# Attention heads taken in pairs, with the masks added by VectorE, in a two-block network on one core

## The chip, the cores and the metric

The kernel runs on one core of a Trainium2 chip. The metric is the device time of one execution in microseconds (us), taken as the median of repeated runs. The engines are named as in the profile: PE is TensorE (matmuls), PEld its weight load, DVE is VectorE, ACT is ScalarE, POOL is GpSimd and SP is the engine that issues most of the DMAs.

## What is computed

Two transformer-like blocks are computed one after the other on 512 tokens of width 1024, in float32. The change touches only the attention of the first block, which has two kinds of heads, eight of each:

```python
def causal_dense_attention(q, k, v, scale):      # 8 heads, d = 96, values of 64
    s = einsum('bqhd,bkhd->bhqk', qi, k) * scale
    s = where(kpos <= qpos, s, NEG_INF)
    p = softmax(s, axis=-1)
    return einsum('bhqk,bkhd->bqhd', p, v)

DIL_PATTERNS = ((128, 1), (512, 4), (2048, 16))
def dilated_attention(q, k, v):                  # 8 heads, d = 64
    for window, dil in DIL_PATTERNS:
        o, lse = banded_causal_attention(strided q, k, v, window // dil)
    w = softmax(stack(lses)); return sum(w * outs)

mix = concatenate([o_mla, o_dil]) @ w_o
x = x + g1 * mix
h2 = rms_norm(x, g_ffn_norm) * (1 + sc2) + sh2   # then a gated FFN, then block 2
mod = silu(c) @ w_ada + b_ada                    # gives sh1, sc1, g1, sh2, sc2, g2
```

The kernel computes the three dilated patterns as one softmax over all keys: a key that lies in k patterns gets the logarithm of k added to its score, and a key that lies in none a large negative number. So both kinds of heads are a score matrix, an additive mask that depends on query and key alone, a softmax, and a product with the values.

## The kernel before, in words

The work before the attention makes the queries and keys transposed (`qT`, `kT` for the causal heads, 96 rows of a head on the partitions; `qd`, `kd` for the dilated heads, where an even head lies on partitions 0 to 63 and the odd one on 64 to 127 of one tile) and the values (`vm`, `vd`). The attention is written as a software pipeline in `block1`: step `n` of 18 makes the scores of head `n`, then transposes the probabilities of head `n-1`, then multiplies those of head `n-2` with the values. A scheduler that builds the program may move instructions of an engine past each other; the order that comes out is fixed when the program is built.

`scores` (lines 404 to 427) works on four query tiles of 128. Tile `i` sees `n = (i+1)*128` keys. L411 is the matmul of queries and keys into a PSUM tile `pp`. A mask matmul then adds the mask into the same tile: for causal heads L708 (an identity matrix times `cmR`, 128 columns, on the diagonal tile alone), for dilated heads L711 and L712 (identity times the high and the low part, `dmH` and `dmL`, of the dilated mask, all `n` columns each). L414 takes the negative row maximum on DVE (`nmax`), L417 the exponential on ACT out of PSUM into SBUF (`probs`), which also gives the row sum `den` by a second ACT instruction; L419 is the reciprocal (`rden`) on DVE. L423 (ACT, tiles 2 and 3) and L425 (DVE, tiles 0 and 1) scale the rows by it.

`probs_T` (lines 429 to 445): ten 128x128 transposes on PE (L438) into three PSUM tiles `aux`, copied to SBUF (`ptr`) by DVE (L441, 512 columns) and ACT (L443, 512 and 256 columns). `attend` (lines 447 to 449): four matmuls (L449, 512, 384, 256 and 128 columns) into 64 partitions of the PSUM tile `pv`, the lower 64 for an even head, the upper 64 for an odd one. After each second head `pv` is split (`split`, L131 on ACT and L132 on DVE) into `mixH` and `mixL`, the two parts that the product with `w_o` (`mm3`, L126 to L128, three matmuls for one product) takes.

All L411, L438 and L449 matmuls are float32 and run as two passes each, so a row of the profile says x2 for one of them, x10 for five transposes' passes, x8 for the four of `attend`. The pools: four PSUM banks for `pp`, three for `aux`, one for `pv`; two `ptr` buffers of 1,280 columns.

Between the heads runs `ada_tiles` (lines 267 to 283), a generator of which each step of the pipeline takes one: it loads 1 MB of `w_ada` (L273, tile `wada`), and DVE multiplies it with a column of silu(c) and adds it to `acc` (L275 for the first of eight, L277 for the others). After eight steps 16 matmuls of one column each (L281, 32 passes) sum `acc` over the partitions, and L282 adds the bias. Two such groups run here. Behind the attention come the small constants of block 2 (`s5_poles`, L898 to L985, mostly DVE on 64x64 tiles), and the product with `w_o` with its weight splits (`wh` by ACT, L131; `wl` by DVE, L132), its evictions (L767) and the first product of the FFN.

Of the kernel before, what the change touches and what calls it, by code (L numbers as in the profile page):

```python
# [11 lines left out]
F32 = mybir.dt.float32  # L12
# [7 lines left out]
P = 128  # L20
# [49 lines left out]
class Kern:  # L70
# [15 lines left out]
    def raw(self):  # L86
        """The next landing place of a weight load."""
# [52 lines left out]
    def rsqrt_act(self, out, ss, n, tag):  # L140
        """out <- (ss / n + EPS) ** -0.5: square root, reciprocal, one Newton step."""
# [11 lines left out]
    def rsqrt_dve(self, out, ss, n, tag):  # L153
        """out <- (ss / n + EPS) ** -0.5 by a bit estimate and three Newton steps."""
# [14 lines left out]
    def later(self, lag, fn):  # L169
        """Queue fn to be traced after the next lag products."""  # L170
# [96 lines left out]
    def ada_tiles(self, c0, n, dst, acc):  # L267
        """dst <- columns c0.. of silu(c) @ w_ada + b_ada, one column per 128; a generator of its steps."""
# [16 lines left out]
    def bcast_rows(self, dst, rstd, n):  # L285
        """dst [P, n*128] <- rstd[:, t] of token t*128+p, on every partition."""
# [8 lines left out]
    def sumsq_add(self, kt, acc, sq, x, e=None):  # L295
        """acc <- acc + x * x, feature tile by feature tile."""
# [7 lines left out]
    def sumsq_rows(self, ps, acc, t0, sizes):  # L304
        """Per token sums over the partitions of acc: column t0 + i of ps for the i-th token tile."""
# [5 lines left out]
    def rstd_rows(self, ps, cols, rb):  # L311
        """rb, on every partition: the reciprocal roots of the mean squares of the tokens in cols; ps: their sums of squares."""
# [17 lines left out]
    def scale_split(self, H, L, x, g):  # L330
        """H, L <- the two parts of x * g, g per partition."""
# [3 lines left out]
    def modulate(self, tiles, src, rb, G, sh, H, L):  # L335
        """H, L <- the two parts of src * rb * G + sh, feature tile by feature tile."""
# [52 lines left out]
    def rope(self, out, x, key, t, heads, rstd):  # L389
        """out, x: [P, heads, d] views; rstd [P, heads]."""  # L390
# [1255 lines left out]
```

## Time and profile before

| | us |
|---|---|
| median of three runs | 1876.71 |
| lowest and highest of them | 1876.2, 1882.28 |
| span of the profiled execution | 1874.8 |
| attention, first score matmul to the first product after the last ones matmuls (216.9 to 346.2) | 129.3 |
| the stretch behind it, up to the transposes of block 2's constants (346.2 to 402.3) | 56.1 |

The profiled execution shows a span of 1874.8 us, from its first to its last instruction; the profile gives no other time of that execution, so what lies around the span is taken as the difference to the median, 1.9 us. In the rows below times are in us from the start of the span; "x8" counts instructions; "idle before" is what the engine waited for. [...]

### The profile page before, as it was taken

What the parts mean: (1) busy time and instruction counts of PE and PEld (TensorE: products, weight loads), DVE (VectorE), ACT (ScalarE), POOL (GpSimd) and SP (SyncE); (2) the same over time, 40 slices, a digit from 0 to 9 for tenths busy, and PEclk for the clock granted to TensorE, in tenths of its full rate; (3) what the DMA queues carried; (4) which work ended last, traced back from release to release, by engine and by line L of the source; (5) the groups of instructions that cost most, each with busy time, mean ns of one, the idle gap of its engine ahead of it and who ended that gap; (6) DMA issues with size and microseconds to landing.
All of it is one profiled execution on the core that took longest, in us unless ns stands there. A gap on an engine that the chain in (4) does not pass through costs nothing. (4 is left out here: it accounts for less than half of the span.)

```text
span 1874.8 us, 28652 instructions
## 1 busy us (share of the span) xinstructions
PE 1796.3 (96%) x11605; PEld 1570.5 (84%) x11605; DVE 1079.9 (58%) x2281; ACT 785.1 (42%) x1290; POOL 320.8 (17%) x440
## 2 busy tenths in 40 slices
PE   1989999999999999999799999999999999999998
PEld 1777765787777777889799999999999999989996
DVE  5697857787543465554488334442444476536652
ACT  3674555345432343333545645342322444324432
POOL 5000000058763861012000000110000000000001
PEclk9899999999999999999899899999999999999999
DMA  7332524343334335355722244824643322332231
GB/s 272 107 111 93 187 91 135 110 78 125 96 112 124 129 116 155 112 188 99 185 74 91 71 135 150 183 97 160 216 139 113 102 91 68 102 107 95 69 102 45
DMA packets 178767, 226.66 MB, mean 121 GB/s; under 512 B 10699, under 2 KB 146746, under 8 KB 175178
## 3 DMA queue, kind: packets, MB, share of 16 engines
q1 hardware_dynamic: 164256, 181.95, 30.6%
q0 software_dynamic: 10640, 38.19, 7.6%
q10 hardware_dynamic: 3738, 4.69, 0.7%
q8 instruction: 91, 1.49, 0.3%
q14 instruction: 42, 0.34, 0.1%
HBM read 196.29 MB, written 32.70 MB: 122 GB/s over the span
## 5 line engine op out<-in xcount | busy, mean ns | idle before, releaser
L126 PE MATMUL pp<-s,wh 128*128 128x258 f32 (+2 forms) x1856 | 533.2, 287 | 2.3 <-DVE st L1206 1.0
L127 PE MATMUL pp<-s,wh 128*128 128x258 f32 (+2 forms) x1856 | 531.6, 286 | 0.0
L128 PE MATMUL pp<-s,wl 128*128 128x258 f32 (+2 forms) x1856 | 529.4, 285 | 0.0
L132 DVE TENSOR_TENSOR wl<-wraw,wh 128x1024 fp32r<-128x1024 f32 (+4 forms) x264 | 307.6, 1178 | 193.8 <-ACT wh L131 192.8
L131 ACT CAST wh<-wraw 128x1024 fp32r<-128x1024 f32 (+4 forms) x264 | 249.1, 965 | 365.9 <-PE pp L127 232.4
L126 PEld LDWEIGHTS pp<-s,wh 128*128 128x128 f32 x1856 | 355.9, 192 | 5.1 <-issue 1.6
L127 PEld LDWEIGHTS pp<-s,wh 128*128 128x128 f32 x1856 | 356.6, 192 | 0.3 <-DVE s L333 0.2
L128 PEld LDWEIGHTS pp<-s,wl 128*128 128x128 f32 x1856 | 356.5, 192 | 0.0
L126 PE MATMUL pp<-h2H,wh 128*128 128x512 f32 x336 | 134.2, 400 | 2.4 <-DVE cy L852 2.4
L127 PE MATMUL pp<-h2L,wh 128*128 128x512 f32 x336 | 133.8, 398 | 0.8 <-DVE h2L L343 0.7
L128 PE MATMUL pp<-h2H,wl 128*128 128x512 f32 x336 | 132.6, 395 | 0.0
L126 PEld LDWEIGHTS pp<-h2H,wh 128*128 128x128 f32 x336 | 63.4, 189 | 20.2 <-ACT aH L131 2.8
L127 PEld LDWEIGHTS pp<-h2L,wh 128*128 128x128 f32 x336 | 63.4, 189 | 16.0 <-DVE h2L L343 2.0
L128 PEld LDWEIGHTS pp<-h2H,wl 128*128 128x128 f32 x336 | 63.6, 189 | 14.4
L126 PE MATMUL pp<-aH,wh 128*128 128x512 f32 x176 | 70.1, 398 | 0.0
L127 PE MATMUL pp<-aL,wh 128*128 128x512 f32 x176 | 69.8, 396 | 0.0
L128 PE MATMUL pp<-aH,wl 128*128 128x512 f32 x176 | 69.8, 396 | 0.0
L1563 POOL TENSOR_TENSOR ht<-ht,gf 128x512 f32<-128x512 f32 x4 | 5.7, 1434 | 344.7 <-ACT fsq L1561 344.7
L126 PE MATMUL pp<-wh,hH 128*128 128x512 f32 (+1 forms) x160 | 62.7, 392 | 1.2 <-ACT hH L519 1.2
L127 PE MATMUL pp<-wl,hH 128*128 128x512 f32 (+1 forms) x160 | 62.2, 388 | 0.5 <-DVE wl L132 0.5
L1527 DVE TENSOR_TENSOR xz<-pp,rb_f 128x516 f32<-128x516 f32 x44 | 30.6, 696 | 54.3 <-PE pp L128 54.3
L128 PE MATMUL pp<-wh,hL 128*128 128x512 f32 (+1 forms) x160 | 61.5, 385 | 0.0
(598 smaller groups left out, 3566.1 us busy)
## 6 DMA issues: line engine op xcount, KB each, us to landing
wraw<-in_w_up_dram SPq DMA_DIRECT2D x40, 1024.0 KB, 5.8
wada<-in_w_ada_dram SPq DMA_DIRECT2D x24, 1024.0 KB, 5.0
wraw<-in_w_in_dram SPq DMA_DIRECT2D x17, 1024.0 KB, 6.0
wraw<-in_w_in_dram SPq DMA_DIRECT2D x26, 512.0 KB, 6.3
wraw<-in_w_down_dram SPq DMA_DIRECT2D x16, 704.0 KB, 4.5
wraw<-in_w_down_dram SPq DMA_DIRECT2D x8, 1024.0 KB
xraw<-MO_d SPq DMA_DIRECT2D x5, 896.0 KB
sg_d<-sg POOLq DMA_DIRECT2D x16, 258.0 KB, 2.4
```

What stands on the lines that cost most here:

```text
L126: mm(ps, lhsT=sh, rhs=mh, start=start, stop=False)
L127: mm(ps, lhsT=sh, rhs=ml, start=False, stop=False)
L128: mm(ps, lhsT=sl, rhs=mh, start=False, stop=stop)
L131: self.nc.scalar.copy(H, x)
L132: self.nc.vector.tensor_tensor(L, x, H.bitcast(F32), ALU.subtract)
L1527: nc.vector.tensor_tensor(xz, ps, rb, ALU.mult)
L1563: nc.gpsimd.tensor_tensor(h, h, gf[:, :512], ALU.mult)
```

## The change

The heads are taken in pairs, so the pipeline has 10 steps. `scores` makes the tiles of the two heads in turn: tile `i` of the first, tile `i` of the second, each into its own `pp` bank. There is no mask matmul. DVE reads the scores from PSUM and the mask from SBUF and writes minus their sum to SBUF, with the running minimum as `nmax` in the same instruction (`tensor_tensor_reduce`); the exponential then reads that SBUF tile in place, with a scale of -1. The causal mask is now a tile of 512 columns of which 384 are zero, the dilated one a single float32 tile. `attend` takes the two heads in turn: the first writes partitions 0 to 63 of `pv`, the second 64 to 127. The `ptr` tiles live in the weight pool, under the tags `wh` and `wl` of the weight splits, and `probs` has four buffers of each size instead of two. Two steps of `ada_tiles` are taken for each pair.

In the diff the comments that were only deleted are left out.

```diff
-    def scores(self, qT, kT, mask):
+    def scores(self, pair, mask):
         nc = self.nc
-        probs = []
+        probs = ([], [])
         for i in range(NT):
             n = (i + 1) * P
-            sc = self.prod()
-            nc.tensor.matmul(sc[:, :n], lhsT=qT[:, i * P : (i + 1) * P], rhs=kT[:, :n], start=True, stop=False)
-            mask(sc, i, n)
-            nm = self.tmp.tile([P, 1], F32, tag="nmax", bufs=8, name=self.nm("nmax"))
-            nc.vector.tensor_reduce(nm, sc[:, :n], AX.X, ALU.max, negate=True)
-            pr = self.att.tile([P, n], F32, tag=f"probs{i}", bufs=2, name=self.nm("probs"))
-            nc.scalar.activation(pr, sc[:, :n], AF.Exp, bias=nm, scale=1.0, accum_out=den)
+            scs = [self.prod() for _ in pair]
+            for (qT, kT), sc in zip(pair, scs):
+                nc.tensor.matmul(sc[:, :n], lhsT=qT[:, i * P : (i + 1) * P], rhs=kT[:, :n], start=True, stop=True)
+            for a, sc in enumerate(scs):
+                nm = self.tmp.tile([P, 1], F32, tag="nmax", bufs=16, name=self.nm("nmax"))
+                pr = self.att.tile([P, n], F32, tag=f"probs{i}", bufs=4, name=self.nm("probs"))
+                nc.vector.tensor_tensor_reduce(pr, sc[:, :n], mask[:, S - n :], -1.0, 3.0e38, ALU.add, ALU.min, nm)
+                nc.scalar.activation(pr, pr, AF.Exp, bias=nm, scale=-1.0, accum_out=den)
...
-    def probs_T(self, probs):
+    def probs_T(self, probs, tag):
-        buf = self.att.tile([P, 10 * P], F32, tag="ptr", bufs=2, name=self.nm("ptr"))
+        buf = self.wpool.tile([P, WCAP], F32, tag=tag, bufs=self.wbufs[1], name=self.nm("ptr"))
...
-    def attend(self, ptr, v, pv, row):
+    def attend(self, ptrs, vs, pv):
         for j in range(NT):
-            self.nc.tensor.matmul(pv[row : row + 64, j * P :], lhsT=v(j), rhs=ptr[j], start=(j == 0), stop=(j == NT - 1))
+            for a in range(2):
+                self.nc.tensor.matmul(pv[64 * a : 64 * a + 64, j * P :], lhsT=vs[a](j), rhs=ptrs[a][j], start=(j == 0), stop=(j == NT - 1), skip_group_check=True)
...
-                cmR = self.att.tile([P, P], F32R, name="cmR")
-                nc.vector.tensor_copy(cmR, cm)
                 nc.vector.tensor_scalar(dm, dm, 0.125, None, ALU.mult)
-                dmH = self.att.tile([P, S], F32R, name="dmH")
-                dmL = self.att.tile([P, S], F32R, name="dmL")
-                self.split(dmH, dmL, dm)
...
-                for n in range(18):
-                    if n < 16:
-                        st[n] = [self.scores(heads[n][0], heads[n][1], heads[n][3])]
+                for n in range(10):
+                    if n < 8:
+                        st[n] = self.scores(pairs[n][0], pairs[n][2])
                         next(ada_rest, None)
-                    if 1 <= n < 17:
-                        st[n - 1] = self.probs_T(st[n - 1][0])
+                        next(ada_rest, None)
+                    if 1 <= n < 9:
+                        st[n - 1] = [self.probs_T(x, tag) for x, tag in zip(st[n - 1], ("wh", "wl"))]
                     if n >= 2:
                         m = n - 2
-                        if m % 2 == 0:
-                            pv = self.psA.tile([P, 512], F32, tag="pv", bufs=1, name=self.nm("pv"))
-                        self.attend(st.pop(m), heads[m][2], pv, m % 2 * 64)
-                        if m % 2:
-                            self.split(mixH[:, m // 2], mixL[:, m // 2], pv)
+                        pv = self.psA.tile([P, 512], F32, tag="pv", bufs=1, name=self.nm("pv"))
+                        self.attend(st.pop(m), pairs[m][1], pv)
+                        self.split(mixH[:, m], mixL[:, m], pv)
```

The diff does not tell in which order the engines now take their work. Three places matter. The first is PE inside the dilated heads. Before, the scores of a head stand with their masks, and `attend` follows for one head (`pp`, `pv` are PSUM tiles, `ptr` the transposed probabilities of one head):

```order
L411 MATMUL pp_692_2941<-kd_1630,qd_1629 128x256
L711 MATMUL pp_692_2941<-dmH_2235,identR_94 128x256
L712 MATMUL pp_692_2941<-dmL_2236,identR_94 128x256
L411 MATMUL pp_697_2952<-kd_1630,qd_1629 128x384
L711 MATMUL pp_697_2952<-dmH_2235,identR_94 128x384
L712 MATMUL pp_697_2952<-dmL_2236,identR_94 128x384
...
L449 MATMUL pv_712_2998<-ptr_683_2907,vd_416 64x512
L449 MATMUL pv_712_2998<-ptr_683_2907,vd_416 64x384
L449 MATMUL pv_712_2998<-ptr_683_2907,vd_416 64x256
```

With the change the same place reads as follows (L412 is the score matmul, L455 that of `attend`):

```order
L455 MATMUL pv_732_2969<-ptr_673_2804,vm_419 64x512
L455 MATMUL pv_732_2969<-ptr_677_2821,vm_419 64x512
L455 MATMUL pv_732_2969<-ptr_673_2804,vm_419 64x384
L455 MATMUL pv_732_2969<-ptr_677_2821,vm_419 64x384
...
L412 MATMUL pp_733_2980<-kd_1630,qd_1629 128x128
L412 MATMUL pp_734_2981<-kd_1630,qd_1629 128x128
L412 MATMUL pp_743_2998<-kd_1630,qd_1629 128x256
L412 MATMUL pp_744_2999<-kd_1630,qd_1629 128x256
```

So the two heads of a pair alternate, each with a row half (scores of dilated heads) or a column half (`attend`) of the array, and 96 mask matmuls are gone.

The second place is DVE at the boundary of two dilated heads, where the steps of `ada_tiles` stand. Before:

```order
L277 SCALAR_TENSOR_TENSOR acc_2239<-wada_3272,csilu,acc_2239 128x2048
L414 TENSOR_REDUCE nmax_3154<-pp_3150 128x1
L414 TENSOR_REDUCE nmax_3165<-pp_3161 128x1
L277 SCALAR_TENSOR_TENSOR acc_2239<-wada_3345,csilu,acc_2239 128x2048
L419 RECIPROCAL rden_3159<-den_3157 128x1
```

With the change, between the sixth and the seventh pair (ISA is the `tensor_tensor_reduce`; a second row of the same name is the read of its running minimum):

```order
L277 SCALAR_TENSOR_TENSOR acc_2234<-wada_2929,csilu,acc_2234 128x2048
L445 COPY ptr_2935<-aux_2942 128x512
L277 SCALAR_TENSOR_TENSOR acc_2234<-wada_2932,csilu,acc_2234 128x2048
L445 COPY ptr_2952<-aux_2959 128x512
L132 TENSOR_TENSOR mixL<-pv_2969,mixH 128x512
L417 ISA probs_2985,nmax_2984<-pp_2980,dm 128x128
L417 ISA nmax_2984 128x1
L417 ISA probs_2992,nmax_2991<-pp_2981,dm 128x128
L417 ISA nmax_2991 128x1
```

The steps now come two by two, after the norms of a pair and around the copies of its `ptr`. The eight steps of the second group stand so behind the dilated pairs: the first (L275) behind the fifth pair, two each behind the sixth, seventh and eighth, and the last behind the last `ptr` copies.

The third place is PE at the end of the attention. Before, 12 of the `w_o` products stood among the transposes of the last heads, and the second group of ones matmuls behind the last `attend`:

```order
L126 MATMUL pp_3599<-mixH,wh_3593 128x512
L438 MATMUL aux_3372<-ident,probs_3303 128x128
...
L449 MATMUL pv_3388<-ptr_3371,vd 64x128
L281 MATMUL aux_3567<-ones,acc_2239 128x1 x16
```

With the change:

```order
L455 MATMUL pv_3276<-ptr_3214,vd 64x128
L281 MATMUL aux_3466<-ones,acc_2234 128x1 x16
L455 MATMUL pv_3287<-ptr_3242,vd 64x512
L455 MATMUL pv_3287<-ptr_3259,vd 64x512
...
L126 MATMUL pp_3498<-mixH,wh_3492 128x512
L127 MATMUL pp_3498<-mixL,wh_3492 128x512
```

So the ones matmuls now stand ahead of the last pair's `attend`, and all `w_o` products behind it. The splits of `w_o` on DVE (`wl`) and ACT (`wh`), of which five and six stood among the last heads, stand behind the attention too, on DVE among the constants of block 2.

## Rows read from the trace of the kernel before

**Rows 1.** The page: span, and busy time of two engines (us, share, instructions).

```profile
span 1874.8 us, 28652 instructions
PE 1796.3 (96%) x11605; PEld 1570.5 (84%) x11605; DVE 1079.9 (58%) x2281; ACT 785.1 (42%) x1290; POOL 320.8 (17%) x440
```

**Rows 2.** Windows: stretch, length, busy PE, PEld, DVE, ACT, POOL, granted clock, DMA share, GB/s.

```profile
216.90:346.20 129.30, 129.30 (x590) 77.93 (x588) 82.03 (x200) 80.40 (x209) 2.65 (x5) 0.97 0.33 114
346.20:402.30 56.10, 56.10 (x240) 44.96 (x239) 50.67 (x158) 17.64 (x24) 14.81 (x9) 0.97 0.30 85
268.30:275.20 6.90, 6.90 (x21) 3.78 (x21) 3.12 (x6) 2.86 (x7) 0.00 (x0) 0.51 0.17 31
```

**Rows 3.** Timeline of PE in one causal head: start us, us, instruction.

```profile
229.68 0.49 PE L411 MATMUL pp<-kT,qT 96*128 96x128 f32 x2
...
232.34 1.26 PE L438 MATMUL aux<-ident,probs 128*128 128x128 f32 x10
233.53 2.37 PE L449 MATMUL pv<-ptr,vm 128*64 128x512 f32 x8
```

**Rows 4.** Timeline of PE in one dilated head.

```profile
292.46 0.48 PE L411 MATMUL pp<-kd,qd 64*128 64x128 f32 x2
292.87 0.33 PE L711 MATMUL pp<-dmH,identR 128*128 128x128 f32 x1
...
295.68 1.12 PE L411 MATMUL pp<-kd,qd 64*128 64x512 f32 x2
296.73 0.50 PE L711 MATMUL pp<-dmH,identR 128*128 128x512 f32 x1
...
297.30 1.25 PE L438 MATMUL aux<-ident,probs 128*128 128x128 f32 x10
298.48 2.37 PE L449 MATMUL pv<-ptr,vd 128*64 128x512 f32 x8
300.78 0.37 PE L411 MATMUL pp<-kd,qd 64*128 64x128 f32 x1
```

**Rows 5.** Groups of DVE instructions in 216.9 to 346.2: busy us, mean ns, idle before.

```profile
L277 DVE SCALAR_TENSOR_TENSOR acc<-wada,csilu,acc 128x2048 f32<-128x2048 f32 x8 | 18.7, 2340 | 0.5 <-DMA wada<-in_w_ada_dram 0.5
L414 DVE TENSOR_REDUCE nmax<-pp 128x1 f32<-128x512 f32 x16 | 10.9, 684 | 4.2 <-PE pp L712 3.6 <-PE pp L708 0.6
L441 DVE COPY ptr<-aux 128x512 f32<-128x512 f32 x16 | 10.9, 682 | 2.7 <-PE aux L438 2.4
L419 DVE RECIPROCAL rden<-den 128x1 f32<-128x1 f32 x64 | 8.9, 154 | 6.6 <-ACT probs L417 6.6
L132 DVE TENSOR_TENSOR wl<-wraw,wh 128x1024 fp32r<-128x1024 f32 x5 | 6.1, 1216 | 1.2 <-ACT wh L131 1.2
```

**Rows 6.** Windows, DVE instructions of L414 alone: length, busy DVE, clock, DMA.

```profile
216.90:346.20 129.30, 30.61 (x64) 0.97 0.33 114
```

**Rows 7.** Groups of ACT instructions in 216.9 to 346.2.

```profile
L417 ACT ACTIVATION_READ_ACCUMULATOR probs<-pp,nmax 128x1 f32 x64 | 12.8, 200 | 0.0
L131 ACT CAST wh<-wraw 128x1024 fp32r<-128x1024 f32 x6 | 6.2, 1052 | 0.0
```

**Rows 8.** Timeline of PE at a short window around 402.27.

```profile
402.27 0.27 PE L983 MATMUL aux<-ident,s_q 64*64 64x64 f32 x2
```

**Rows 9.** Timeline of PE: the first ones matmuls, and the end of the attention.

```profile
265.30 4.05 PE L281 MATMUL aux<-ones,acc 128*128 128x1 f32 x32
...
334.34 0.51 PE L126 MATMUL pp<-mixH,wh 128*128 128x512 f32 x1
...
337.68 0.40 PE L128 MATMUL pp<-mixH,wl 128*128 128x512 f32 x1
...
339.59 3.07 PE L449 MATMUL pv<-ptr,vd 128*64 128x384 f32 x14
...
346.19 0.48 PE L126 MATMUL pp<-mixH,wh 128*128 128x512 f32 x1
```

**Rows 10.** DMA issues in 300 to 350: instruction, KB each, us from issue to landing.

```profile
wraw<-in_w_o_dram SPq DMA_DIRECT2D x4, 1024.0 KB, 5.0
```

More of the change, by code (lines that the diff above doesn't have):

```diff
@@ L428, in probs_T @@
-    def probs_T(self, probs):
+            scs = [self.prod() for _ in pair]
[5 more added lines that the diff above has]
+                nc.vector.tensor_tensor_reduce(pr, sc[:, :n], mask[:, S - n :], -1.0, 3.0e38, ALU.add, ALU.min, nm)
+                den = self.tmp.tile([P, 1], F32, tag="den", bufs=16, name=self.nm("den"))
+                nc.scalar.activation(pr, pr, AF.Exp, bias=nm, scale=-1.0, accum_out=den)
+                rd = self.tmp.tile([P, 1], F32, tag="rden", bufs=16, name=self.nm("rden"))
+                nc.vector.reciprocal(rd, den)
+                probs[a].append((pr, rd))
@@ L430, in probs_T @@
+        for i in range(NT):
+            for a in range(2):
+                pr, rd = probs[a][i]
+                if i in self.act_norm:
+                    nc.scalar.activation(pr, pr, AF.Copy, scale=rd)
+                else:
+                    nc.vector.tensor_scalar(pr, pr, rd, None, ALU.mult)
+        return [[pr for pr, _ in x] for x in probs]
+    def probs_T(self, probs, tag):
         nc = self.nc
-        buf = self.att.tile([P, 10 * P], F32, tag="ptr", bufs=2, name=self.nm("ptr"))
+        buf = self.wpool.tile([P, WCAP], F32, tag=tag, bufs=self.wbufs[1], name=self.nm("ptr"))
@@ L445, in probs_T @@
         return out
[L447 removed]
+    def attend(self, ptrs, vs, pv):
         for j in range(NT):
[L449 removed]
+            for a in range(2):
+                self.nc.tensor.matmul(pv[64 * a : 64 * a + 64, j * P :], lhsT=vs[a](j), rhs=ptrs[a][j], start=(j == 0), stop=(j == NT - 1), skip_group_check=True)
     def block1(self):
@@ L695, in block1 @@
             with tc.tile_pool(name="att", bufs=1, reuse_waits="tile") as self.att:
-                cm = self.att.tile([P, 10 * P], F32, tag="ptr", bufs=2, name="cm")[:, :P]
-                nc.scalar.dma_start(cm, A["k_cm"])
-                dm = self.att.tile([P, 10 * P], F32, tag="ptr", bufs=2, name="dm")[:, :S]
+                cm = self.att.tile([P, S], F32, name="cm")
+                nc.gpsimd.memset(cm[:, : S - P], 0.0)
+                nc.scalar.dma_start(cm[:, S - P :], A["k_cm"])
+                dm = self.att.tile([P, S], F32, name="dm")
@@ L717, in block1 @@
-                for h in range(8):
-                    heads.append((qT[:96, h], kT[:96, h], lambda j, h=h: vm[:, j, h * 64 : h * 64 + 64], causal))
-                for h in range(8):
-                    r = slice(h % 2 * 64, h % 2 * 64 + 64)
-                    heads.append((qd[r, h // 2], kd[r, h // 2], lambda j, h=h: vd[:, j, h * 64 : h * 64 + 64], dilm))
+                pairs = []
+                for h in range(0, 8, 2):
+                    pairs.append(([(qT[:96, h + a], kT[:96, h + a]) for a in range(2)], [lambda j, h=h + a: vm[:, j, h * 64 : h * 64 + 64] for a in range(2)], cm))
@@ L722, in block1 @@
+                for h in range(0, 8, 2):
+                    r = [slice(a * 64, a * 64 + 64) for a in range(2)]
+                    pairs.append(([(qd[r[a], h // 2], kd[r[a], h // 2]) for a in range(2)], [lambda j, h=h + a: vd[:, j, h * 64 : h * 64 + 64] for a in range(2)], dm))
                 st = {}
-                for n in range(18):
-                    if n < 16:
-                        st[n] = [self.scores(heads[n][0], heads[n][1], heads[n][3])]
+                for n in range(10):
+                    if n < 8:
+                        st[n] = self.scores(pairs[n][0], pairs[n][2])
```

16 lines of the change are left out of this document (removed).

## The prediction

> **What bounds the kernel now.** I read the page first [rows 1]: PE is busy in 96% of the span, DVE in 58%. An average over stages does not say what the attention is bound by, so the next view is the windows [rows 2]. In the attention, 216.9 to 346.2, PE is busy for all 129.3 us; DVE is busy for 82.0 and ACT for 80.4. In the stretch behind, PE is again never idle, and DVE is near its limit there, with 50.7 of 56.1 us. So PE work that is taken out of the attention shortens it, until DVE or ACT comes next; the reader is to see that both stand at about two thirds.
>
> The timelines of PE give the price of a head. A causal head: scores with masks from 229.68 to 232.34, 2.66 us; ten transposes to 233.53, 1.19 [rows 3]; attend 2.30 (298.48 to 300.78, the same shapes) [rows 4]. Together 6.15, a pair 12.3. A dilated head goes from 292.46 to 300.78, 8.32 us, a pair 16.6; its scores with masks are 4.84 of it [rows 4].
>
> **What the change does to PE.** The masks go. A causal score block then has 1,280 columns in two passes, like an attend block, so I take 2.30 for it. For a dilated one the starts give 0.41 us for the first tile and 1.05 for the last [rows 4]; the cost grows evenly with columns, so four tiles are four times the mean, 2.92.
>
> Pairing lets two matmuls share the array. For column halves (attend) the trace has two pieces of evidence. Two 64x64 transposes on different halves show as one stretch of 0.27 us [rows 8]. And the 14 passes from 339.59 are six of head 14 (1,536 columns) and eight of head 15 (2,560), in other halves; at 2.30 per 2,560 columns they would take 3.68 one after the other, and took 3.07 [rows 9]. So I take 2.30 for the attend of a pair, bounded by 4.60 if nothing overlaps. Of two full-width matmuls on row halves no row shows anything: the scores of a dilated pair are bounded by 2.92 (together) and 5.84 (in turn). With the transposes, 2.38, PE needs:
> - causal pair: 4.60 + 2.38 + 2.30 = 9.3 (11.6 with attend in turn), 12.3 before;
> - dilated pair: 2.92 + 2.38 + 2.30 = 7.6, or 10.5 with scores in turn, or 12.8 with both in turn; 16.6 before.
>
> **What it does to DVE and ACT.** DVE's 82.0 us less the accumulations (18.7) and the weight splits (6.1) leave 57.2, or 7.15 per pair [rows 2, 5]. Of that the row maxima are 30.6, 3.83 per pair [rows 6]. I price the new instruction like the maximum that it replaces, since it streams the same columns once: the accumulation with two float32 SBUF inputs takes 2340 ns for 2,048 columns, 1.14 ns each, no more than the maximum's 684 for 512, 1.34 each [rows 5]. New is the second row per tile, the read of the minimum. No row shows it on DVE; the bounds are nothing and the 200 ns of ACT's accumulator read [rows 7], and I take the reciprocal's 154 ns [rows 5], DVE's own instruction on one column: 8 x 0.154 = 1.2. So DVE needs 8.4 per pair (7.15 to 8.75). Two accumulations add 4.7 in the sixth to eighth pair: 13.1, and DVE is the bound there. The two copies of the last pair and the last accumulation are left over at the end: 2 x 0.68 + 2.34 = 3.7.
>
> ACT's 80.4 less the casts of weights (6.2) are 9.3 per pair [rows 2, 7]; reading SBUF in place of PSUM is taken at nothing, since ACT is behind DVE where DVE bounds, and level with PE elsewhere. The constants' preparation (a memset of 384 columns on POOL, three small operations fewer on DVE and ACT) is off the path: POOL is busy for 2.65 us in all of the attention [rows 2]. The `ptr` tiles in the weight slots cost nothing while no weight needs the slot; the first `w_o` splits need one, and by then the pair that held it, the sixth, has been read.
>
> **The sum.** From 216.9: 1.3 us until the first scores have reached DVE (an estimate: a first matmul of 0.49 [rows 3] and the start of a maximum). Four causal pairs at 10.0: PE and ACT at 9.3 each and DVE at 8.4 are so near each other that I add 0.7 for handing over. [...] Three pairs at 13.1 + 0.5 for handing over: 40.8. Then 3.7. That is 216.9 + 1.3 + 40.0 + 13.5 + 40.8 + 3.7 = 316.2. Behind it stand the second ones matmuls, 3.6 us (342.6 to 346.19), and the last pair's attend, 2.30: the products with `w_o` start at 322.1. Before they go on at 346.19, with twelve already done among the last heads; those twelve, less six transposes' passes at 0.12, took 2.9 of the time from 334.34 to 338.0 [rows 9]. So the comparable start was 343.3, and the gain is 21.2 us.
>
> Behind the attention PE has the same products as before. DVE gets more there: the five splits of `w_o` that it had done earlier, 6.1 us, and an eviction. But it starts 6 us ahead of the products, at 316, and can do small constants in that time; 50.7 + 6.9 - 6 = 51.6 still fits in 56.1. The load that the first split waits for takes 5.0 us [rows 10], two casts 2.1 [rows 7], two splits 2.4; it can be issued when the accumulations of the eighth pair free the landing place, near 312, so it is ready at about 321.5, just ahead of its use. I take the stretch behind at no loss.
>
> The profiled execution has a span of 1874.8, and 1.9 us lie around it to the median of 1876.71; the gain is taken off the median: 1876.7 - 21 = **1856**. With the low ends (causal pairs at 9.3, the fifth at 11.5, no read of the minimum and no handing over, 7.15 + 4.68 = 11.8 in the last three) the gain is 31: 1845. With the high ends (causal 11.6, the fifth pair 16, 3 us lost in the stretch behind) it is 9: 1868.
>
> **The rivals.**
> 1. *The halves do not overlap.* Causal pairs take 11.6 (+6.4), the fifth some 3 more, the last attend 2.3 more; dilated pairs at 12.8 stay under DVE's 13.6. Gain 9: **1867**. For it: no row of two 128-column halves that start together for their whole length. Against: rows 8 and 9 as above. Chance 0.10.
> 2. *The stretch behind becomes DVE's.* If the `w_o` loads or splits come late, or the constants cannot use the head start, up to 6.9 us come back: **1863**. For it: DVE at 50.7 of 56.1 [rows 2]. Against: the head start. Chance 0.12.
> 3. *Slower: the new DVE instruction at half rate.* Place: the path from scores to exponential, which every tile takes. DVE would carry 3.83 us more per pair: 12.2 in causal pairs, 13.0 with handing over (+12), the fifth +3.5, the last three 17.4 each (+11.5). In all +27: **1883**. It decides from where a tile's mean goes from 0.48 us (30.6 over 64 [rows 6]) to some 0.8, since the gain of 21 is 2.6 us per pair. For it: an operation that no row shows, with two inputs and a written tile. Against: the two-input accumulation at 1.14 ns per column [rows 5]. Chance 0.09. [...]
> 4. *No change: evacuation keeps the old pace.* ACT and DVE hand each tile on four times (minimum, exponential, norm, copy), in order on both engines, and a tile that is late stops the other head's too. If these handovers stretch the pairs to the old 12.3 and 16.6, PE only idles where it worked: **1876**. For it: PE, ACT and DVE all within 1 us in the causal pairs. Against: DVE has whole pairs of slack now, with 82.0 of 129.3 [rows 2], and four `probs` buffers. Chance 0.09. [...]
> 5. *PE, no longer full, is granted the lower clock in the dilated pairs.* At 0.51 they would need 15 to 21 us of PE in place of 13.6; with the middle, +16: **1872**. The only stretches at 0.51 that I read stand behind ones matmuls [rows 2]. Chance 0.05.
>
> **How the numbers follow.** 0.3% of this time, about what a measurement can tell from no change, is 5.6 us. My forecast (1845 to 1868) has a chance of 0.55; with rivals 1, 2 and 5 faster has 0.82. Same is rival 4, 0.09; slower is rival 3, 0.09. A range from 1843 to 1871 takes in the forecast's bounds and rivals 1 and 2, and leaves out 3, 4 and most of 5.
>
> **What would show it.** In the profile of the changed kernel: rows of the two heads' attend that start together; scores of a dilated pair within 3 us if row halves overlap; the new instruction near 0.68 us for 512 columns, its second row near 0.15; PE idle between 217 and 320 and DVE close to full from the sixth pair on; causal pairs every 10 us, the last dilated ones every 13.6; the first `w_o` product near 322; block 2's transposes (L983 before, at 402.27) near 381. Wrong would be: the instruction near 1 us or more, pairs no shorter than before, or a stretch behind of more than 60 us.

## The result, and the profile after

The changed kernel took 1845.78 us (median of 4 runs, 1842.11 to 1854.98) against 1876.45 for the kernel before: ratio 0.985, 95% interval 0.982 to 0.988. Run again beside more runs of before it took 1847.21 (6 runs) against 1874.86 (19 runs), 0.9845 [0.9818, 0.9871]. So the gain is 28 to 31 us; the prediction had 21 and the range 1843 to 1871. One of the six executions of the experiment e5 below took 6466.6 us at a mean granted clock of 0.44 (clocks are shares of full speed) and is left out of its row in the table.

The profiled execution was the longest of its four, 1854.98 with a span of 1853.0. A second profile of the same kernel (the experiment e1) has a span of 1839.0 and is of the shortest of its six executions. Both are read below; where they differ, a difference of that size between two profiles shows nothing of a change. First the page of the changed kernel, the rows that answer to [rows 1]:

```profile
span 1853.0 us, 28507 instructions
PE 1759.5 (95%) x11509; PEld 1547.9 (84%) x11509; DVE 1076.4 (58%) x2343; ACT 783.6 (42%) x1289; POOL 321.5 (17%) x441
```

The page hardly differs: the change lies in one stage of 130 us. The windows show it. The columns are those of [rows 2]; the stretches are the attention (first score to first `w_o` product), the stretch behind it, and the rest. The changed kernel:

```profile
218.85:322.69 103.84, 91.42 (x482) 54.56 (x480) 77.51 (x274) 74.57 (x204) 2.69 (x5) 0.87 0.35 123
322.69:380.00 57.31, 57.31 (x252) 46.27 (x252) 52.48 (x148) 22.13 (x29) 15.07 (x9) 1.00 0.40 120
379.90:1853.00 1473.10, 1441.64 (x9936) 1307.35 (x9935) 785.84 (x1421) 581.40 (x818) 270.58 (x379) 0.97 0.39 117
```

The same kernel in e1:

```profile
218.11:317.69 99.58, 90.12 (x482) 54.77 (x480) 76.27 (x274) 74.10 (x204) 2.69 (x5) 0.88 0.36 126
317.69:374.90 57.21, 57.21 (x251) 46.20 (x249) 52.49 (x148) 22.12 (x29) 15.08 (x9) 1.00 0.41 120
374.90:1838.90 1464.00, 1431.33 (x9936) 1297.95 (x9935) 785.18 (x1421) 580.72 (x818) 270.58 (x379) 0.98 0.40 118
```

The attention goes from 126.4 (129.3 less the 2.9 of the twelve `w_o` products in it [rows 2, 9]) to 103.8 and 99.6; the stretch behind from 59.0 with those products to 57.3. PE now idles for 9 to 12 us of the attention, and its granted clock there falls from 0.97 to 0.87 and 0.88. The rest, work that the change does not touch, differs by 9.1 us between two executions of one kernel, at clocks of 0.97 and 0.98; before, it took 1472.5. Single spans therefore say less than medians, and less than the attention alone.

The timeline of PE in the changed kernel has the prices of a pair, as [rows 3, 4] had those of a head:

```profile
252.79 2.38 PE L455 MATMUL pv<-ptr,vm 128*64 128x512 f32 x16
255.09 0.92 PE L412 MATMUL pp<-kd,qd 64*128 64x128 f32 x6
...
270.24 0.93 PE L412 MATMUL pp<-kd,qd 64*128 64x128 f32 x8
271.10 0.87 PE L442 MATMUL aux<-ident,probs 128*128 128x128 f32 x6
271.90 2.10 PE L412 MATMUL pp<-kd,qd 64*128 64x384 f32 x8
273.93 1.31 PE L442 MATMUL aux<-ident,probs 128*128 128x128 f32 x10
```

The 16 passes of two heads' `attend` go from 252.79 to 255.09, 2.30 us, as long as the eight passes of one head before: the column halves overlap fully. The 16 score passes of a dilated pair take 0.86 + 2.03 = 2.89, which is the forecast's 2.92. One head alone takes 2.36, though (e5 below), so the row halves overlap for 1.8 us of 2.36 and not fully. (The x6 and x10 of the transposes, L442, count transposes: there are ten a head, each one row, and not five of two passes.) The DVE groups answer to [rows 5]:

```profile
L277 DVE SCALAR_TENSOR_TENSOR acc<-wada,csilu,acc 128x2048 f32<-128x2048 f32 x8 | 18.7, 2342 | 2.3 <-DMA wada<-in_w_ada_dram 2.3
L417 DVE CUSTOM_DVE_ANT_0 probs<-pp,cm 128x512 f32<-128x512 f32 x8 | 5.5, 682 | 1.9 <-PE pp L412 1.9
L417 DVE CUSTOM_DVE_ANT_0 probs<-pp,dm 128x512 f32<-128x512 f32 x8 | 5.4, 675 | 0.0
L417 DVE DVE_READ_ACCUMULATOR2_ANT nmax<- 128x1 f32 x64 | 5.3, 83 | 0.0
```

The instruction that adds the mask and keeps the minimum takes 682 ns for 512 columns, the maximum took 684; its second row, the read of the minimum, takes 83. That row costs DVE no time of its own: the window of both rows together, which answers to [rows 6], has 30.0 us for 128 rows, and the 64 maxima had 30.6.

```profile
218.85:322.69 103.84, 30.00 (x128) 0.87 0.35 123
```

The next windows, of the dilated pairs in e1, show who is the bound there:

```profile
272.11:278.11 6.00, 4.04 (x34) 2.74 (x30) 6.00 (x7) 5.17 (x13) 0.00 (x0) 1.00 0.39 127
...
284.11:290.11 6.00, 3.54 (x23) 2.08 (x21) 6.00 (x8) 4.19 (x10) 0.00 (x0) 0.97 0.37 123
...
296.11:302.11 6.00, 3.23 (x22) 2.04 (x18) 6.00 (x11) 4.99 (x12) 0.00 (x0) 0.82 0.28 66
302.11:308.11 6.00, 5.21 (x18) 2.86 (x20) 5.05 (x6) 1.01 (x3) 0.52 (x1) 0.50 0.80 296
```

In the first three DVE is full and PE busy for 3.2 to 4.0 of 6 us. In the two stretches left out between them DVE is busy for 5.1 and 4.5 us and PE for 5.7 and 6.0. Behind the last of them the granted clock is 0.50.

### The profile page after: what moved, and what is told of

Same layout as the page of the kernel before. It is cut to its first block, busy times and chain, and to the rows that moved or that the text cites. A ratio compares the mean times of both kernels' runs of the same rounds, so it can differ in the third digit from the quotient of the medians.

```text
span 1853.0 us, 28507 instructions
## 1 busy us (share of the span) xinstructions
PE 1759.5 (95%) x11509; PEld 1547.9 (84%) x11509; DVE 1076.4 (58%) x2343; ACT 783.6 (42%) x1289; POOL 321.5 (17%) x441
## 5 line engine op out<-in xcount | busy, mean ns | idle before, releaser
L1521 DVE TENSOR_TENSOR xz<-pp,rb_f 128x516 f32<-128x516 f32 x44 | 30.6, 696 | 54.3 <-PE pp L128 54.3
```

Source lines behind the costliest of these rows:

```text
L1521: nc.vector.tensor_tensor(xz, ps, rb, ALU.mult)
```

## The experiments

The attention is measured from the first score to the first `w_o` product in one profile each; in e3 and e10 the last `attend` stands behind the first 12 and 14 of those products, and the stretch goes on to the product behind it. The time is the median of n runs, the ratio is to before on the same chip.

| run | us (n) | ratio [95%] | attention, clock in it |
|---|---|---|---|
| e1, the change unaltered | 1847.2 (6) | 0.9845 [0.9818, 0.9871] | 99.6, 0.88 |
| e2, DVE masks, heads singly | 1863.9 (8) | 0.9937 [0.991, 0.9963] | 120.5, 0.89 |
| e3, pairs, mask matmuls | 1880.5 (12) | 1.003 [1.0005, 1.0055] | 132.3, 0.88 |
| e4, attend in turn | 1848.8 (6) | 0.9861 [0.9826, 0.9896] | 103.4, 0.95 |
| e5, scores in turn | 1846.1 (5) | 0.9844 [0.9814, 0.9875] | 100.2, 0.92 |
| e12, both in turn | 1850.9 (8) | 0.9871 [0.9843, 0.9898] | 113.4, 0.91 |
| e11, half of the modulation left out | 1829.5 (6) | 0.9769 [0.974, 0.9798] | 88.8, 0.94 |
| e6, two accumulations later | 1844.0 (5) | 0.9845 [0.982, 0.9869] | 97.1, 0.93 |
| e8, half of eight accumulations on POOL | 1844.6 (5) | 0.9849 [0.9823, 0.9876] | 99.8, 0.90 |
| e9, e6 and e8 | 1844.3 (4) | 0.9845 [0.982, 0.9869] | 96.9, 0.91 |
| e10, second group early | 1856.8 (6) | 0.991 [0.9884, 0.9935] | 114.6, 0.85 |
| e13, half of the second group in the FFN | 1858.3 (6) | 0.9896 [0.9865, 0.9928] | not the same work |

### The change again, and each half of it alone

e1 is the kernel unaltered.

> The changed kernel once more, for its spread. The four runs so far lie between 1842.1 and 1855.0 with mean granted clocks from 0.976 down to 0.967, and the profiled one was the slowest. Theory A: the spread is TensorE's lower clock level, granted for more or fewer stretches in the attention where PE now idles; then this profile shows a different number of half-clock stretches between 217 and 323, its span differs from 1853 by about half the difference of their lengths (between 2 and 10 us), and the work outside the attention takes the same time. Theory B: the spread comes from another stage; then the first product with w_o stands within 2 us of 322.7 whatever the span is.

It confirmed the time; its windows stand above. Neither theory holds by itself: of the 14.0 us between the two spans 4.3 lie in the attention, where the first profile has a late load and a clock of 0.52 from 224.11 to 230.11 (e1: 1.00), and 9.1 behind the stretch after it. e2 is the kernel before with the masks on DVE and no other change:

```diff
-            mask(sc, i, n)
-            nc.vector.tensor_reduce(nm, sc[:, :n], AX.X, ALU.max, negate=True)
+            nc.vector.tensor_tensor_reduce(pr, sc[:, :n], mask[:, S - n :], -1.0, 3.0e38, ALU.add, ALU.min, nm)
```

> The kernel before with one part of the change: VectorE adds the masks with the running minimum, heads still one by one, no pairs. Theory A (PE is the bound, so each part is worth the PE time it removes, until DVE is next): a causal head goes from 6.15 to 2.30 + 1.19 + 2.30 = 5.8, a dilated one from 8.32 to 2.92 + 1.19 + 2.30 = 6.4; in all 3 + 15 = 18 us, so about 1858; DVE needs 4.2 per head and 6.5 with an accumulation, so it is level with PE in the dilated heads and 3 us of the gain may be lost. Rival (pairing adds nothing, because the softmax on DVE and ACT sets the pace once the masks are gone): as fast as the whole change, about 1846.

e3 is the changed kernel with the mask matmuls, the maximum and an exponential that reads PSUM:

```diff
+                mask(sc, i, n)
...
-                nc.vector.tensor_tensor_reduce(pr, sc[:, :n], mask[:, S - n :], -1.0, 3.0e38, ALU.add, ALU.min, nm)
+                nc.vector.tensor_reduce(nm, sc[:, :n], AX.X, ALU.max, negate=True)
...
-                nc.scalar.activation(pr, pr, AF.Exp, bias=nm, scale=-1.0, accum_out=den)
+                nc.scalar.activation(pr, sc[:, :n], AF.Exp, bias=nm, scale=1.0, accum_out=den)
```

> The changed kernel with the masks back as matmuls on PE and the maximum and exponential reading PSUM, but with heads in pairs. Theory A: the attend of a pair takes 2.3 in place of 4.6, eight times, 18 us; the score matmuls of the two heads are no longer next to each other (the mask matmuls stand between them), so row halves save nothing: about 1858. Rival (halves save little, the masks were the gain): 1870 or more.

The masks alone are worth 11 us, the pairs alone nothing or a small loss, both together 28. The parts do not add, and both expectations (1858 each) were missed. The windows of the attention, e2:

```profile
217.60:338.13 120.53, 114.66 (x482) 66.96 (x480) 76.51 (x262) 75.29 (x205) 2.66 (x5) 0.89 0.30 103
```

and e3, `w_o` products among it as before:

```profile
217.16:349.43 132.27, 128.75 (x590) 80.26 (x588) 83.66 (x211) 76.08 (x206) 2.66 (x5) 0.88 0.30 105
```

Busy PE times granted clock is an estimate of the work at full clock: before 129.3 x 0.97 = 125, e3 128.75 x 0.88 = 113, e2 114.66 x 0.89 = 102. By this estimate pairing took some 12 us of PE work out, and PE was busy as long as ever, at a clock of 0.88 for 0.97. In e3 a score tile also keeps its `pp` bank until the exponential has read it, which the timeline of PE shows:

```profile
221.02 0.91 PE L412 MATMUL pp<-kT,qT 96*128 96x384 f32 x2 [1.98 <-ACT probs L420]
```

Such waits come to only 2.6 us in all, so the clock is the larger part of why pairs alone brought nothing; I did not hold the clock fixed, which leaves this argued.

### What the shared array is worth

e4 puts the `attend` matmuls of the two heads in turn, e5 the scores, e12 both:

```diff
-        for j in range(NT):
-            for a in range(2):
+        for a in range(2):
+            for j in range(NT):
```

> The changed kernel with one edit: attend does all four matmuls of the first head, then those of the second, so column halves do not alternate. Theory A (PE and ACT set the pace in the causal pairs, DVE in the dilated ones): 2.3 us more in each of four causal pairs and the last one, nothing in the others: about +9 to +11, 1855 to 1858, if the clock were the same; but PE idles less, so fewer half-clock stretches may give back up to 5. Rival (the softmax sets the pace in all pairs): +2 us, the last pair alone, 1848.

```diff
-        for i in range(NT):
+        for a, i in itertools.product(range(2), range(NT)):
```

> The changed kernel with the scores of a pair made head by head (four tiles of the first, then four of the second), so that row halves do not alternate in the dilated pairs. Theory A (DVE with its accumulations sets the pace from the sixth pair on): a dilated pair's scores take 5.8 in place of 2.9 on PE; only the fifth pair, which PE bounds, pays it, +3 us, and PE idles less in the others, which may raise the granted clock and give some of it back: 1845 to 1851. Rival (PE bounds the dilated pairs too): +2.9 in each of four, +12: 1859.

> The changed kernel with neither the scores nor the attend of the two heads in turn, so that the array is not shared (beyond the boundary of the two heads); the heads are still in pairs and the masks on VectorE. Each of the two alone cost 1 to 3 us. Theory A (each was hidden behind ACT in the causal and DVE in the dilated pairs, and PE would be next): PE needs 5.8 and 6.4 us per head as with masks on VectorE and single heads, so the loss of both is more than the sum of each: 1852 to 1864. Rival (sharing the array is worth nothing; pairs with masks on VectorE give the whole gain): 1845 to 1850.

The time of e5 is that of e1. Its timeline of PE has the scores of one dilated head by themselves, from 278.32 to 280.68:

```profile
278.32 2.42 PE L412 MATMUL pp<-kd,qd 64*128 64x128 f32 x8
280.68 2.21 PE L442 MATMUL aux<-ident,probs 128*128 128x128 f32 x16
```

So a pair in turn takes 4.7 us, not the 5.8 that the expectation and the prediction had; sharing saves 1.8 of them, 7 us over the four pairs.

The timeline of PE in e4 has the price of `attend` in turn, 249.62 to 253.48, 3.86 us for 2.30; not 4.60. The missing 0.74 us are some 800 columns at 2.30 us per 2,560, about the last two pieces of the first head (768 columns in two passes); counted back from 253.48 by 2.30, the other head, on the other half, begins at 251.18, so its first piece runs beside them:

```profile
249.62 3.93 PE L455 MATMUL pv<-ptr,vm 128*64 128x512 f32 x16
253.48 0.92 PE L412 MATMUL pp<-kd,qd 64*128 64x128 f32 x6
```

Eight pairs at 1.56 are 12.5 us of PE, yet the kernel's time can't be told from that of the change. The window shows where they went:

```profile
217.17:320.60 103.43, 96.20 (x482) 56.38 (x480) 77.44 (x274) 74.64 (x204) 2.69 (x5) 0.95 0.36 124
```

By the same estimate e4 has 96.20 x 0.95 = 91 us of work at full clock and e1 90.12 x 0.88 = 79 (the first profile 91.42 x 0.87 = 80): the 12 us are there. In busy time only 5 to 6 are left of them. Of the attention's length nothing can be said: 103.4 in e4, 99.6 and 103.8 in the two profiles of the change. That PE is granted less because it idles more is argued, not shown; e6 below shares the array as the change does and was granted 0.93 in its profile.

With both in turn (e12) the median is 3.7 us above e1 (5 by the ratios) and the intervals overlap; its profile is of its longest execution, so its 113.4 is too long. In e12 the overlap is not all gone, since the heads still meet at the borders of `attend`: 8 x 1.56 + 4 x 1.8 = 20 us of sharing are undone, of 8 x 2.30 + 4 x 1.8 = 26. What those 20 are worth, some 4 us or nothing, was not resolved. Against e2, whose heads go one by one, e12 is 13 us faster: most of what pairing brings on top of the masks is not the sharing but the order, two heads' chains on the engines at once, with the deeper buffers, the steps and the splits that go with it. No run takes these apart.

### What bounds the dilated pairs

In e11 half of the modulation is left out, the second group's accumulations, which are cut to 64 of 2,048 columns:

```diff
+                m = 64 if c0 > 2048 else n
...
-                nc.vector.scalar_tensor_tensor(acc[:, :n], raw[:, :n], self.csilu[:, kt : kt + 1], acc[:, :n], ALU.mult, ALU.add)
+                nc.vector.scalar_tensor_tensor(acc[:, :m], raw[:, :m], self.csilu[:, kt : kt + 1], acc[:, :m], ALU.mult, ALU.add)
```

> The changed kernel with the second group's accumulations cut to 64 of their 2,048 columns after the first, so that half of the modulation is left out; DVE carries 15 us less in the sixth to eighth pair and POOL nothing. It measures what those accumulations cost. Theory A (DVE bounds those pairs): 12.5 per pair falls to about 9.3, ACT's load, and the last one no longer holds the ones matmuls: 10 us less, 1836. Rival (handovers): 3 us or less, 1843 or more.

The time falls by 17.7 us from e1 by the medians, by 14 by the ratios; the two profiled executions are 10.7 apart, all of it in the attention. The windows go from the first score of the sixth pair to that of the seventh, from there to that of the eighth, and from there to the second ones matmuls. First e1, then e11:

```profile
265.15:272.38 7.23, 7.23 (x49) 4.26 (x49) 6.35 (x31) 5.79 (x20) 0.00 (x0) 1.00 0.09 37
272.38:284.85 12.47, 10.17 (x65) 5.94 (x63) 11.55 (x33) 10.35 (x29) 0.00 (x0) 1.00 0.47 168
284.85:309.95 25.10, 19.09 (x89) 10.61 (x88) 20.84 (x43) 13.87 (x36) 0.52 (x1) 0.73 0.51 172
```

```profile
266.17:275.21 9.04, 8.24 (x53) 4.86 (x52) 7.35 (x33) 7.60 (x23) 0.00 (x0) 1.00 0.22 73
275.21:284.14 8.93, 8.14 (x54) 4.58 (x53) 7.13 (x33) 8.93 (x27) 0.00 (x0) 1.00 0.66 243
284.14:299.38 15.24, 14.93 (x96) 8.89 (x95) 10.22 (x40) 12.46 (x35) 0.52 (x1) 1.00 0.76 289
```

The accumulations stand behind the norms of their pair. So in e1 the sixth pair's stretch is still PE's, at 7.2 us; the next holds two accumulations and takes 12.5, with DVE busy for 11.55; the last holds the other five and takes 25.1, at a clock of 0.73. Without them the stretches take 9.0, 8.9 and 15.2, DVE needs 7.2 for a pair, and PE or ACT is near the bound. (The order of PE differs a little, so compare the sums: 44.8 us and 33.2, DVE busy for 38.7 and 24.7.) The profile puts PE's waits in e1's attention down to ACT's copies of `ptr` (7.4 us) rather than to DVE's (0.8); but e11 takes only DVE work out. So DVE's accumulations set these stretches, as the prediction had it, and they are the next thing to move. How much of the 11.6 us is waiting and how much the clock (0.73 in e1's last stretch, 1.00 in e11's) was not taken apart.

### Trying to move them

e6 gives the first group's last two accumulations a scalar that hangs on the first pair's minimum, so that DVE takes the first pair's scores ahead of them:

```diff
+                nc.vector.scalar_tensor_tensor(acc[:, :n], raw[:, :n], (self.cs2 if c0 == 2048 and kt >= 6 else self.csilu)[:, kt : kt + 1], acc[:, :n], ALU.mult, ALU.add)
...
+                            nc.vector.scalar_tensor_tensor(self.cs2, self.nm_last.to_broadcast([P, 8]), 0.0, self.csilu, ALU.mult, ALU.add)
```

> The changed kernel with the last two accumulations of the first group on DVE made to depend on the first pair's running minimum, so that they no longer stand, waiting for their loads, ahead of the first row minimum. Theory A (in the first profiled run the wait of 2.3 us for a load held DVE, so PE idled for 3.0 us and was granted the half clock for 6.8): no profile of this kernel has a gap of PE over 1 us in the first pair nor a half-clock stretch there; median 0 to 4 us below that of the changed kernel, 1843 to 1847. Rival (the two accumulations cost the same 4.7 us in pairs two and three, where DVE needs 8.4 of 9.3): no gain, or 2 us slower.

It was meant for a wait that the first profile of the changed kernel has and e1 has not. Here is DVE's timeline of the first profile, with an accumulation that waited for its load and held the first minimum up:

```profile
220.81 2.35 DVE L277 SCALAR_TENSOR_TENSOR acc<-wada,csilu,acc 128x2048 f32<-128x2048 f32 x1 [2.26 <-DMA wada<-in_w_ada_dram]
223.08 0.28 DVE L417 CUSTOM_DVE_ANT_0 probs<-pp,cm 128x128 f32<-128x128 f32 x1
```

PE stood for 3.0 us, and the granted clock over 222.9 to 229.7 was 0.51. e6 has no such gap in its first pair, and an attention of 97.1, but its interval is that of the change. e8 gives half the columns of the second group to POOL, e9 is both:

```diff
+                    nc.gpsimd.tensor_scalar(raw[:, h:n], raw[:, h:n], self.csilu[:, kt : kt + 1], None, ALU.mult)
+                    nc.gpsimd.tensor_tensor(acc[:, h:n], acc[:, h:n], raw[:, h:n], ALU.add)
```

> The changed kernel with half of the columns of the second group's accumulations moved from DVE to POOL, which is idle there. Theory A (in the sixth to eighth pair DVE is the bound, and the wait of PE for copies is a wait for DVE): 1.17 us less per accumulation, two per pair and one at the end, so 8 us less, and fewer half-clock stretches as PE idles less, up to 5 more: 1834 to 1839. Rival one (the pace there is set by the handovers of transposes and copies between PE, ACT and DVE): less than 3 us. Rival two (POOL's work slows DVE's instructions, or POOL comes last before the ones matmuls): no gain or slower, with DVE's instructions longer than 0.68 us for 512 columns or the ones matmuls waiting for POOL.

> Both of the last two edits together. Theory A: the two act in different pairs, so the gains add: 1830 to 1837, and faster than both kernels. Rival: as the better of the two alone, or no better than the changed kernel.

Neither is faster than the change, and e9 is no better than either. DVE was to lose 9 us of work and lost none: its busy time in the attention is 81.1 in e8 and 76.3 in e1. The timeline of e8, DVE:

```profile
275.74 1.27 DVE L278 SCALAR_TENSOR_TENSOR acc<-wada,csilu,acc 128x1024 f32<-128x1024 f32 x1
...
285.03 3.46 DVE L278 SCALAR_TENSOR_TENSOR acc<-wada,csilu,acc 128x1024 f32<-128x1024 f32 x1
```

and POOL:

```profile
285.04 2.36 POOL L284 TENSOR_TENSOR acc<-acc,wada 128x1024 f32<-128x1024 f32 x1
```

The same DVE instruction takes 1.27 us once, and 3.46 where POOL's 2.36 starts with it: it ends 1.1 us after POOL's has ended, so it seems to have stood while that ran. What kept them apart no run shows, and which of the two started first can't be told from starts 0.01 us apart.

e10 keeps e6's edit and spreads the second group's steps forward, beginning in the causal pairs:

```diff
+                        for _ in range((4, 5, 2, 2, 2, 2, 1, 0)[n]):
+                            next(ada_rest, None)
```

> The late steps of before, and the generator's steps taken earlier: 4, 5, 2, 2, 2, 2, 1 and 0 for the eight pairs in place of two for each, so that the second group's accumulations stand in the second to seventh pair, where DVE has room (27 of 35 us busy up to the first ones matmuls), and the second ones matmuls ahead of the last pair. Theory A (the accumulations on DVE are what the sixth to eighth pairs wait for; moving half of them to POOL did not help since DVE's own instructions then took up to 3.5 us): up to 7 us off the attention's 97, fewer half-clock stretches: 1835 to 1841. Rival (the pace of the dilated pairs is set by the handovers of copies and norms whatever DVE carries): 1843 to 1846, as with late steps alone.

It lost 10 us to e1 and 13 to e6. The ones matmuls moved with the steps, and PE, in its fixed order, met them ahead of the accumulations that they need (timeline of PE, in brackets the idle time and its releaser):

```profile
234.36 6.99 PE L281 MATMUL aux<-ones,acc 128*128 128x1 f32 x32 [2.38 <-DVE acc L277]
...
293.81 6.96 PE L281 MATMUL aux<-ones,acc 128*128 128x1 f32 x32 [4.09 <-DVE acc L277]
```

They then took 7.0 us each; in the first profile of the change the second ones took 3.82 (314.98 to 318.80) at a granted clock of 0.95. That the clock makes the difference is an estimate: e10's is shown only as a mean, 0.85 over its attention. e13 keeps e6 and moves half of the second group (1,024 columns) into the FFN, in four pieces of 256 columns behind a generator of its own:

```diff
+                ada_rest = itertools.chain(self.ada_tiles(2048, 2048, mod[:, 16:32], acc), self.ada_tiles(4096, 1024, mod[:, 32:40], acc))
...
+                        next(ada_late, None)
+                        next(ada_late, None)
```

> The late steps of before, and the second group of accumulations cut to the 1,024 columns that the products behind the attention need (the scale of the FFN's norm); the other 1,024, the gate g2 that is first read after the first half of the FFN's up products, are computed during those, in four pieces of 256 columns, on DVE as before. Nothing of the computation is left out. Leaving out all of the second group took some 16 us off. Theory A (DVE's accumulations bound the sixth to eighth pair): half of that, 7 to 8 us, with DVE near half idle in the FFN: attention 89 to 93 us after its first score, median 1835 to 1840, faster than both kernels. Rival (the loads and ones matmuls in the FFN hold PE there, or lower its clock): the stretch after the attention gets longer by what the attention gains, 1843 to 1848.

The attention shortened as meant: first score to second ones matmuls 84.1 us, 91.1 in e6. The FFN's start gave back more: the time is 14 us above that of e6 (10 by the ratios). Both profiles are of the longest execution of their kernel. The windows there, e6:

```profile
400.00:450.00 50.00, 45.63 (x194) 33.86 (x192) 35.28 (x38) 22.84 (x36) 42.91 (x55) 0.93 0.35 115
```

and e13:

```profile
400.00:450.00 50.00, 38.56 (x156) 28.39 (x155) 45.71 (x59) 22.04 (x35) 38.18 (x51) 0.86 0.39 125
```

DVE has 10 us more there and PE 7 us less, with 38 matmul rows fewer and a clock of 0.86 for 0.93; where the rest of the loss lies was not traced. No version that computes everything is clearly faster than the changed kernel.

## Why the prediction was right, and where its sizes were off

The gain of 28 to 31 us lies at the low end that the forecast worked out (31), not at its middle. The mechanism held; several terms were off, and some of them made up for one another.

- *The masks leave PE, DVE carries them at no price.* Right: 682 ns for 684. Rival 3, half rate, is refuted. The read of the minimum was a term too many: I took 154 ns a tile, 1.2 us a pair, and its row of 83 ns adds nothing to DVE's busy time (30.0 us for 30.6). So DVE needs 7.2 us per pair and not 8.4 (76.3 less 18.7 over eight pairs in e1, and the same in e11).
- *Halves overlap.* Right for `attend`: 2.30 a pair. For the scores of a dilated pair 2.89 met 2.92, but by luck: my price of a head, taken between mask matmuls, was too high (2.36 in e5), and the overlap is not full. Rival 1's mechanism is refuted. Its price of 11 us was wrong as well: e12, which undoes three quarters of the sharing, lies 4 to 5 us above e1 and is not clearly apart from it. In turn a dilated pair needs 4.7 + 2.4 + 3.9 = 11 us of PE, still under the 12.5 that DVE takes.
- *Causal pairs every 10 us.* Mis-sized, too long: they come every 9.0 (one `attend` at 243.77, the next at 252.79 in the first profile). And from the first score to the first ones matmuls I had 1.3 + 40.0 + 2.9 = 44.2; e1 took 34.9, the first profile 40.9 with the late load:

```profile
218.11:253.00 34.89, 33.74 (x174) 20.29 (x172) 27.25 (x130) 34.62 (x101) 2.18 (x4) 1.00 0.31 115
```

  Ahead of the ones matmuls PE's order has the scores of all five pairs, but the transposes of three and the `attend` of two: 4 x 4.60 + 2.92 + 3 x 2.38 + 2 x 2.30 = 33.1 us, where I counted four whole pairs. And ACT, busy for 34.62 of 34.89, loses nothing between its instructions: the 0.7 a pair that I added for handing over is not there.
- *Dilated pairs DVE's, 13.6 each.* Right in mechanism, and in the sum by luck: from the sixth pair's first score to the second ones matmuls I had 3 x 13.6 + 3.7 = 44.5, and e1 took 44.8, but as 7.2, 12.5 and 25.1 (windows above). The sixth pair had no accumulation yet, the read of the minimum cost nothing, and the end was 8 us longer than I had. The fifth pair was too short as well. No run shows the 13.5 that the sum has for it: it is my estimate, 7.6 of PE work and 3.9 for the ones matmuls (265.30 to 269.20 before), which make the 11.5 of the low end, and 2.0 more for the 0.51 that stood behind them there [rows 2]. From the first ones matmuls to the sixth pair it leaves 13.5 - 2.9 = 10.6; e1 took 12.2, at a clock of 0.72:

```profile
252.97:265.15 12.18, 12.18 (x65) 8.38 (x63) 5.71 (x24) 7.03 (x21) 0.00 (x0) 0.72 0.22 69
```

  At the end the last pair's transposes wait for copies of ACT and DVE around the accumulations, and then `attend` takes longer, as the timeline of PE in e1 shows:

```profile
284.85 0.93 PE L412 MATMUL pp<-kd,qd 64*128 64x128 f32 x8
...
299.17 0.66 PE L442 MATMUL aux<-ident,probs 128*128 128x128 f32 x4 [2.02 <-ACT ptr L447]
...
305.49 4.54 PE L455 MATMUL pv<-ptr,vd 128*64 128x512 f32 x16
309.95 3.88 PE L281 MATMUL aux<-ones,acc 128*128 128x1 f32 x32
313.76 4.00 PE L455 MATMUL pv<-ptr,vd 128*64 128x512 f32 x16
317.69 0.51 PE L126 MATMUL pp<-mixH,wh 128*128 128x512 f32 x1
```

  An `attend` pair of 2.30, at a clock of 1.00 (252.79 to 255.09 in the first profile), takes 4.46 and 3.93 here. In the first profile the same two take 4.46 and 3.89, at 0.50 (310.52 to 314.98) and 0.58 (318.80 to 322.69).
- *The lower clock (rival 5).* It came, though the time did not go as far as 1872: the clock in the attention is 0.88, and by the estimate above a full clock would spare PE 11 us of 90, part of them in waits. It was no alternative to my sum but a tax within it. The sum had it for the fifth pair alone (the 2.0 us); the stretch at the end, where `attend` takes 4.5 and 3.9 for 2.3 (at 0.50 and 0.58), belonged in it too.
- *The stretch behind at no loss.* Right, with a gain of 1.8: 57.2 for 59.0 (rows above and [rows 2, 9]), all of it at a clock of 1.00. Before, the clock was 0.97 there [rows 2], which by an estimate is 1.7 of 56.1 us, so most of the gain is the clock's. Rival 2 is refuted; DVE has 52.5 of 57.2, the forecast was 51.6.
- *The sum.* First `w_o` product forecast at 322.1, found at 322.7 and 317.7; block 2's transposes forecast near 381, found at 379.9 and 374.9. In e1 the attention is 5.6 shorter than forecast (105.2) and the stretch behind 1.8: 21.2 + 7.4 = 28.6, of which 1.2 went since the first score stood at 218.11 for 216.90; between the medians it is 27.7. Rival 4, the old pace, is refuted with it.

Open: which activity of PE decides the clock in these stretches, what part of the order makes the pairs pay, and whether the 4 us of the shared array are real. A PE kept busy through DVE's stretches by other products was not tried.

## What to carry to other kernels

Price PE work that is removed by the engine that comes next and by the clock, not by its own length: here 12 us of `attend` moved the median by 1.5, inside the intervals. Taking work off the full engine and interleaving two independent chains paid 28 us together, 11 and nothing alone, so test the parts alone before crediting either. When a sum comes out, check its stages one by one: here two of them were wrong by 6 and 8 us in opposite directions. Work moved to a free engine or a later stage was not free here: with half of eight accumulations on POOL, DVE was busy for 81.1 us in the attention, 76.3 without (e8, e1), and with half of the second group's columns in the FFN PE was busy for 7 us less of 50 there (e13, e6). Look for an instruction that grows by about the length of one on the other engine, as from 1.27 us to 3.46 beside 2.36.

## What the runs showed that I had not expected

- A DVE accumulation that started with a POOL addition, both on SBUF, took 3.46 us for 1.27, with 2.36 on POOL (e8).
- The read of the running minimum has a row of 83 ns and adds nothing to DVE's busy time.
- Heads that stand in turn in e4 still overlapped at their border, on other halves: 3.86 for 4.60.
- PE saved work and was granted less clock: 0.95 in e4 and 0.88 in e1 (0.87 in the first profile), the same instructions in another order. But 0.93 in e6, so the order of the halves is not all of it.
- The same untouched instructions behind the attention took 1464.0 to 1476.9 us (e1 and e6), and the kernel before ran from 1865.5 to 1884.6 over 19 runs; half a per cent between single executions is no effect.
